# Taking GpSimd out of block 2's recurrent branch and attention on one Trainium2 core

## The chip, the cores and the metric

The kernel runs on one core of one Trainium2 chip. The metric is the device time of one execution in microseconds. TensorE (PE) does matmuls and transposes, VectorE (DVE) and ScalarE (ACT) do element-wise work and read PSUM, GpSimd (POOL) does element-wise work on SBUF, and SyncE (SP) issues DMAs. Each engine works through its own queue in order.

## The reference, cut to what matters

Two first blocks (a pooled branch and latent attention) and one second block run over 512 tokens of width 1024; 16 meta tokens are added for the first two blocks. The change lies in the second block, in the recurrent branch and in the differential attention:

```python
# recurrent branch, for each direction (forward, reverse)
r = sigmoid(x @ w_a + b_a); i = sigmoid(x @ w_i + b_i)
log_a = -8 * r * softplus(-lam)
a = exp(log_a)
u = sqrt(-expm1(2 * log_a)) * (i * x)
h = scan(h = a * h + u);  y = (h_fwd + h_bwd) * gelu(lru_g)
# attention: 8 heads, two sub-heads of 64 each
q = rope(rms_norm(q)); k = rope(rms_norm(k))
p = softmax(q0 k0 / 8) - lam * softmax(q1 k1 / 8)
o = rms_norm(p @ v) * (1 - lam_init)
# then: gates * (o @ w_attn_o, y @ w_lru_o), w_out, and a mixture of 16 experts
```

## The kernel before, in words

**Precision.** Every fp32 product is made of three matmuls: the operands are split into a rounded high part (a cast on ScalarE, L145 for weights, names `wh`, `xH`) and a low part (a subtraction on VectorE, L146, names `wl`, `xL`); `mm3` (L151 to L153) issues high x high, high x low, low x high. Outputs land in PSUM tiles `mm`.

**Order.** The program is written as one stream, and the framework's list scheduler orders each engine's queue ahead of time, by priority and by its own idea of when operands are ready. Buffers of a pool are handed out in turn, so a new tile waits until the old one in its buffer has been read. Independent projections are written as Python generators of steps (`fill`), and `next(fill)` puts a step of them between pieces of the recurrent branch and of the attention. Below they are called fillers: matmuls that PE can do while a chain through other engines is under way.

**The recurrent branch** (L1011 to L1055) runs in 4 groups of 2 units. A unit splits its input `xr` into `rH` (ScalarE) and `rL` (VectorE, L1024), computes four gate products into PSUM (`sc`, `tr`, `pv`), and then, in each of two directions: Tanh of both gates (L1034, L1035), Exp to the decay `la` (L1036), another Tanh (L1037), the square of the decay `a2` (L1039, GpSimd), and (a2 + 1) * m2 on VectorE (L1040). L1041 makes the input term. A group ends with the square roots on ScalarE (L1047, behind a load of the function table), and with L1049, two scans (L1050, L1051) and the sum of both directions `hs` (L1052, GpSimd) on each unit. The fillers here are the steps of `qkv2` for heads 0 to 3 and of `lru_g` (L1003 to L1008).

**qkv2** (L1240 to L1286) computes k, q and v for four heads. For each 128 tokens of k and q, ScalarE squares the PSUM result, VectorE sums (L1264), multiplies by the rotary cosine (L1265, `kt` or `qt`) and by the sine with halves exchanged (L1266, `rt`), and GpSimd adds both (L1270). The PSUM bank is free after L1266.

**Attention** (L1288 to L1357) goes over 8 heads, in two rounds of four. A head transposes k and q (L1304, PE, into PSUM `tr`) and splits them: ScalarE copies the high part (L1306, 64 partitions at a time), VectorE subtracts the low part (L1308, `kl` or `q`). For k, both parts are needed on the other 64 partitions too: GpSimd copies `kh` (L1310) and `kl` (L1311) across. Then, for each of four blocks of 128 queries: scores of two sub-heads (L1326, L1327, PSUM `sc`), the maximum (L1328), Exp with a running sum (L1330), the combination (L1331 to L1333), the transposition of the probabilities (L1336) and its copy `pT` (L1338), the product with v (L1340, PSUM `pv`), its scaling `ot` (L1341) and its squares `junk` (L1343). The head ends with a norm over the four blocks (L1346 to L1348, with the 11 small VectorE instructions of `rsqrt`, L169 to L176), a transposition (L1350) and the split of `o` (L1353, L1354). `ps_tr` and `ps_pv` have one bank each; `ps_sc` has two in the first round and four in the second. Fillers of the first round are `lru_o` (operands `lH`, `lL`) and qkv2 for heads 4 to 7; of the second, the gates `g_lru` and `g_attn` (operands `x2H`, `x2L`). Behind the last head come `w_attn_o` (`mm<-o`), `w_out`, the router and the experts.

Of the kernel before, what the change touches and what calls it, by code (L numbers as in the profile page):

```python
# [11 lines left out]
F32 = mybir.dt.float32  # L12
# [4 lines left out]
AF = mybir.ActivationFunctionType  # L17
ALU = mybir.AluOpType
AX = mybir.AxisListType

P = 128
D = 1024
KD = D // P
SEQ = 512
# [110 lines left out]
class Builder:  # L135
# [779 lines left out]
    def block2(self, xH, xL, squares, out):  # L915
        nc, A, tc = self.nc, self.A, self.tc
        V, S, E = nc.vector, nc.scalar, nc.tensor
        with ExitStack() as ctx:
# [15 lines left out]
            sp = sm.tile([P, 16], F32, name="sp")  # L934
# [15 lines left out]
            V.tensor_scalar(t, t, 0.0, 0.5, op0=ALU.max, op1=ALU.mult)  # L950
            V.tensor_tensor(sp, sp, t, op=ALU.add)
            spm = {}
            for f in (-8.0, 8.0):
                spm[f] = sm.tile([P, 16], F32, name=f"sp{int(f) + 16}")
                V.tensor_scalar(spm[f], sp, f, None, op0=ALU.mult)
            hb = {}
            for w in ("a", "i"):
# [37 lines left out]
            hs = Later(self, "hs", 8, SEQ)  # L995
# [18 lines left out]
            for grp in range(4):  # L1014
                wH, wL = [t.rearrange("p (n m c) -> p n m c", n=2, m=4) for t in wl.get(grp)]
                units = []
                for nn in range(2):
                    n = 2 * grp + nn
                    rH = med.tile([P, SEQ], F32R, name="rH", tag="hl")
                    rL = med.tile([P, SEQ], F32R, name="rL", tag="hl")  # L1020
                    ix = med.tile([P, 2, SEQ], F32, name="ix", tag="pr")
                    a, m2 = self.pair("la", F32, (P, 2, SEQ)), self.pair("lm", F32, (P, 2, SEQ))
                    S.copy(rH, xr[n])
                    V.tensor_tensor(rL, xr[n], rH.bitcast(F32), op=ALU.subtract)  # L1024
                    for dd in range(2):
                        u = 8 * dd + n
                        if dd == 0:
                            pr, pi = [self.ps_sc.tile([P, SEQ], F32, name="sc") for _ in range(2)]
                        else:
                            pr = self.ps_tr.tile([P, SEQ], F32, name="tr")  # L1030
                            pi = self.ps_pv.tile([P, SEQ], F32, name="pv")
                        self.mm3(pr, wH[:, nn, 2 * dd], wL[:, nn, 2 * dd], rH, rL, True, True)
                        self.mm3(pi, wH[:, nn, 2 * dd + 1], wL[:, nn, 2 * dd + 1], rH, rL, True, True)
                        S.activation(m2[:, dd], pr, AF.Tanh, scale=0.5, bias=hb["a"][:, u:u + 1])  # L1034
                        S.activation(ix[:, dd], pi, AF.Tanh, scale=0.5, bias=hb["i"][:, u:u + 1])  # L1035
                        S.activation(a[:, dd], m2[:, dd], AF.Exp, scale=spm[-8.0][:, u:u + 1], bias=spm[-8.0][:, u:u + 1])  # L1036
                        S.activation(m2[:, dd], m2[:, dd], AF.Tanh, scale=spm[8.0][:, u:u + 1], bias=spm[8.0][:, u:u + 1])  # L1037
                        a2 = med.tile([P, SEQ], F32, name="a2", tag="pT", bufs=2)
                        nc.gpsimd.tensor_tensor(a2, a[:, dd], a[:, dd], op=ALU.mult)  # L1039
                        V.scalar_tensor_tensor(m2[:, dd], a2, 1.0, m2[:, dd], op0=ALU.add, op1=ALU.mult)  # L1040
                    V.scalar_tensor_tensor(ix, ix, 1.0, xr[n][:, None, :].to_broadcast([P, 2, SEQ]),  # L1041
                                           op0=ALU.add, op1=ALU.mult)
                    units.append((n, a, m2, ix))
                zero = sm.tile([P, 1], F32, name="zero", bufs=2)
                V.tensor_scalar(zero, units[-1][2][:, 1, :1], 0.0, None, op0=ALU.mult)
                for n, a, m2, ix in units:
                    S.activation(m2, m2, AF.Sqrt, scale=0.25, bias=zero)  # L1047
                for n, a, m2, ix in units:
                    V.tensor_tensor(ix, ix, m2, op=ALU.mult)  # L1049
                    V.tensor_tensor_scan(hs[n], a[:, 0], ix[:, 0], 0.0, op0=ALU.mult, op1=ALU.add)  # L1050
                    V.tensor_tensor_scan(m2[:, 1, ::-1], a[:, 1, ::-1], ix[:, 1, ::-1], 0.0, op0=ALU.mult, op1=ALU.add)  # L1051
                    nc.gpsimd.tensor_tensor(hs[n], hs[n], m2[:, 1], op=ALU.add)  # L1052
                for _ in range(5 if grp < 2 else 4):
                    next(fill, None)

# [173 lines left out]
    def qkv2(self, b, wi, xH, xL, inv, epsx, out):  # L1229

        nc = self.nc
        V, S = nc.vector, nc.scalar
        sm, med = self.sm, self.med
        if b == 0:
            self.rope2_tables()
        for w in ("k", "q", "v"):
            tl = []
            for j in range(0, 4, 2):
                t = self.pair(w + "t", F32, (P, 2, SEQ))
                tl += [t[:, 0], t[:, 1]]  # L1240
            out[w] = tl
            pss = [self.psum() for _ in range(4)]
            for i in range(4):
                wH, wL = [t.rearrange("p (k c) -> p k c", k=2) for t in wi[w].get(4 * b + i)]
                for j in range(4):
                    ts = slice(j * P, (j + 1) * P)
                    for kk in range(2):
                        k = 2 * i + kk
                        self.mm3(pss[j], xH[k][:, ts], xL[k][:, ts], wH[:, kk], wL[:, kk], k == 0, k == KD - 1)
                if i < 3:  # L1250
                    yield
            if w != "v":
                ss = sm.tile([P, 4, 8], F32, name="ss" + w)
            for j in range(4):
                ps = pss[j]
                if w == "v":
                    S.activation(tl[j], ps, AF.Copy, scale=inv[:, j:j + 1])
                    continue
                sq = med.tile([P, SEQ], F32, name="sq_", tag="th")
                rt = med.tile([P, SEQ], F32, name="rt_", tag="z", bufs=3)  # L1260
                p8 = ps.rearrange("p (s c) -> p s c", s=8)
                t8 = tl[j].rearrange("p (s c) -> p s c", s=8)
                S.activation(sq, ps, AF.Square)
                V.tensor_reduce(ss[:, j], sq.rearrange("p (s c) -> p s c", s=8), axis=AX.X, op=ALU.add)  # L1264
                V.tensor_tensor(t8, p8, self.TC2[w][:, j, None, :].to_broadcast([P, 8, 64]), op=ALU.mult)  # L1265
                V.tensor_tensor(rt.rearrange("p (s h c) -> p s h c", s=8, h=2),  # L1266
                                ps.rearrange("p (s h c) -> p s h c", s=8, h=2)[:, :, ::-1],
                                self.TS2[w][:, j].rearrange("p (h c) -> p h c", h=2)[:, None].to_broadcast([P, 8, 2, 32]),
                                op=ALU.mult)
                nc.gpsimd.tensor_tensor(tl[j], tl[j], rt, op=ALU.add)  # L1270
            if w == "v":
                yield
                continue
            r = sm.tile([P, 4, 8], F32, name=f"r{w}{b}")
            V.scalar_tensor_tensor(ss, ss, 1.0 / 64, epsx[:, :, None].to_broadcast([P, 4, 8]), op0=ALU.mult, op1=ALU.add)
            self.rsqrt(r, ss, [P, 4, 8], sm)
            if w == "q":
                V.tensor_scalar(r, r, 0.125, None, op0=ALU.mult)
                out["f"] = r
            else:  # L1280
                for j in range(4):
                    t8 = tl[j].rearrange("p (s c) -> p s c", s=8)
                    V.tensor_tensor(t8, t8, r[:, j, :, None].to_broadcast([P, 8, 64]), op=ALU.mult)
            yield

    def attention2(self, b, qkv, lneg, gs, out):  # L1286
# [4 lines left out]
        nc = self.nc  # L1291
        V, S, E = nc.vector, nc.scalar, nc.tensor
        sm, med = self.sm, self.med
        qt, kt, vt, rq = qkv["q"], qkv["k"], qkv["v"], qkv["f"]
        halves = (slice(0, 64), slice(64, P)), (slice(64, P), slice(0, 64))
        for hh in range(4):
# [4 lines left out]
            for src, t2 in ((kt, KH), (qt, QS)):  # L1301
                pt = self.ps_tr.tile([P, SEQ], F32, name="tr")
                for j in range(4):
                    E.transpose(pt[:, j * P:(j + 1) * P], src[j][:, hh * P:(hh + 1) * P], self.ident)  # L1304
                for c, (own, other) in enumerate(halves):
                    S.copy(t2[own, c], pt[own])  # L1306
                    low = KL[c][own] if t2 is KH else t2[other, c]
                    V.tensor_tensor(low, pt[own], t2[own, c].bitcast(F32), op=ALU.subtract)  # L1308
                    if t2 is KH:
                        nc.gpsimd.tensor_copy(t2[other, c], t2[own, c])  # L1310
                        nc.gpsimd.tensor_copy(KL[c][other], low)  # L1311
            po = self.ps_pv.tile([P, 4, P], F32, name="pv")
            ot = med.tile([P, 4, P], F32, name="ot")
            so = sm.tile([P, 4], F32, name="so", bufs=2)
# [515 lines left out]
```

## Time and profile before

| | |
|---|---|
| median of 3 runs | 1806.4 us (1805.15 to 1806.85) |
| profiled execution, its own time | 1805.66 us |
| its span | 1803.9 us |
| PE busy | 1737.3 us, 96% |
| VectorE busy | 1215.6 us, 67% |
| ScalarE busy | 926.4 us, 51% |
| GpSimd busy | 263.1 us, 15% |

The span is the time between the first and the last instruction that the profile shows; 1.76 us of the execution lie around it. Busy shares are averages over stages with different limits. The recurrent branch lies between 940 and 1092 us of the span, the heads between 1090 and 1388 us, and the experts fill 1520 to 1750 us. A listed duration of an instruction is a little longer than the distance between two that follow each other without a gap, since their ends overlap; a sum over a queue goes by the distance. A wait is put down to the engine and line that released it last.

### The profile page before, as it was taken

The page shows a single profiled execution, that of the slowest core. Times are in us where ns is not written, and L with a number is a line of the kernel's source. Part 1 is how long each engine was busy: PE and PEld are TensorE (multiplying, and loading weights), DVE is VectorE, ACT ScalarE, POOL GpSimd, SP SyncE. Part 2 cuts the span into 40 slices and gives each one's busy share as a digit, 9 for nine tenths or more (in the row PEclk, how much of TensorE's full clock was granted, in tenths as well). Part 3 has the DMA queues.
Part 4 walks back from the last instruction along what each step waited for, and adds up shares of the span by engine and source line. Part 5 has one row for each costly group of instructions (what it writes and reads, how often), then busy time and mean ns, then how long its engine had stood idle before and what let it go on. Part 6 is the DMA issues. An engine that isn't in the chain of part 4 may idle for free. (4 is left out here: it accounts for less than half of the span.)

```text
span 1803.9 us, 25746 instructions
## 1 busy us (share of the span) xinstructions
PE 1737.3 (96%) x9706; PEld 1464.3 (81%) x9706; DVE 1215.6 (67%) x2265; ACT 926.4 (51%) x1546; POOL 263.1 (15%) x255
## 2 busy tenths in 40 slices
PE   7999999999999999999999899999999997999997
PEld 7889899999976888888877677777787886888885
DVE  7485555456357555446598988586776539999996
ACT  5343244434434334433337665545565335888885
POOL 4102400001210320000203321021101031111111
PEclk9999999999999999999999999999999998999999
DMA  4122111223322122213532221222124568999995
GB/s 146 59 89 71 49 56 67 77 77 136 116 77 93 53 71 69 72 61 101 181 108 71 82 93 71 70 70 71 47 71 163 190 210 300 383 384 386 381 383 161
DMA packets 69089, 244.36 MB, mean 135 GB/s; under 512 B 10848, under 2 KB 20064, under 8 KB 57056
## 3 DMA queue, kind: packets, MB, share of 16 engines
q1 hardware_dynamic: 64352, 225.89, 34.6%
q0 software_dynamic: 4608, 16.78, 3.7%
q8 instruction: 78, 1.28, 0.3%
q14 instruction: 51, 0.42, 0.1%
HBM read 225.20 MB, written 17.37 MB: 134 GB/s over the span
## 5 line engine op out<-in xcount | busy, mean ns | idle before, releaser
L145 ACT CAST wh<-raw 128x1024 fp32r<-128x1024 f32 (+2 forms) x206 | 212.3, 1031 | 412.9 <-PE mm L152 332.3
L146 DVE TENSOR_TENSOR wl<-raw,wh 128x1024 fp32r<-128x1024 f32 (+2 forms) x206 | 253.6, 1232 | 101.7 <-ACT wh L145 99.8
L151 PE MATMUL mm<-xH,wh 128*128 128x264 f32 (+1 forms) x912 | 291.3, 320 | 11.5 <-ACT xH L361 9.4
L152 PE MATMUL mm<-xL,wh 128*128 128x264 f32 (+1 forms) x912 | 291.1, 320 | 1.3 <-DVE xL L362 1.3
L153 PE MATMUL mm<-xH,wl 128*128 128x264 f32 (+1 forms) x912 | 290.0, 319 | 0.0
L146 DVE TENSOR_TENSOR wl<-we,wh 128x1024 fp32r<-128x1024 f32 x192 | 227.5, 1221 | 15.2 <-ACT wh L145 13.6
L145 ACT CAST wh<-we 128x1024 fp32r<-128x1024 f32 x192 | 198.6, 1050 | 47.6 <-PE mm L153 30.3
L151 PEld LDWEIGHTS mm<-xH,wh 128*128 128x128 f32 x912 | 173.7, 191 | 24.7 <-ACT xH L361 9.4
L152 PEld LDWEIGHTS mm<-xL,wh 128*128 128x128 f32 x912 | 173.9, 191 | 12.2 <-DVE xL L362 2.2
L153 PEld LDWEIGHTS mm<-xH,wl 128*128 128x128 f32 x912 | 173.9, 191 | 10.3
L151 PE MATMUL mm<-wh,eH 128*128 128x512 f32 x256 | 104.2, 407 | 0.0
L151 PE MATMUL mm<-x2H,wh 128*128 128x512 f32 x256 | 102.2, 399 | 0.0
L152 PE MATMUL mm<-x2L,wh 128*128 128x512 f32 x256 | 101.9, 398 | 0.0
L153 PE MATMUL mm<-x2H,wl 128*128 128x512 f32 x256 | 101.8, 398 | 0.0
L153 PE MATMUL mm<-wh,eL 128*128 128x512 f32 x256 | 101.0, 395 | 0.0
L152 PE MATMUL mm<-wl,eH 128*128 128x512 f32 x256 | 100.7, 393 | 0.0
L126 POOL TENSOR_TENSOR z<-z,sq 128x528 f32<-128x528 f32 (+1 forms) x26 | 43.4, 1670 | 331.1 <-DVE wl L146 230.7
L151 PE MATMUL mm<-wh,x2H 128*128 128x512 f32 x192 | 77.0, 402 | 4.8 <-DVE rt__9342 L1266 2.8
L153 PE MATMUL mm<-wh,x2L 128*128 128x512 f32 x192 | 76.1, 400 | 0.0
L152 PE MATMUL mm<-wl,x2H 128*128 128x512 f32 x192 | 76.1, 396 | 0.0
L789 ACT ACTIVATE pr<-sc,bi,r3q 128x264 f32<-128x264 f32 (+3 forms) x80 | 46.6, 590 | 54.9 <-DVE bi L787 54.2
L151 PE MATMUL mm<-mgH,wh 128*128 128x264 f32 (+1 forms) x192 | 61.7, 321 | 0.0
(625 smaller groups left out, 4051.6 us busy)
## 6 DMA issues: line engine op xcount, KB each, us to landing
we<-in_w_moe SPq DMA_DIRECT2D x192, 512.0 KB
raw<-in_w_out SPq DMA_DIRECT2D x12, 1024.0 KB
raw<-in_w_g_mla SPq DMA_DIRECT2D x8, 1024.0 KB
raw<-in_w_g_pool SPq DMA_DIRECT2D x8, 1024.0 KB
raw<-in_w_c_q SPq DMA_DIRECT2D x6, 1024.0 KB
raw<-in_w_q_b SPq DMA_DIRECT2D x6, 768.0 KB
raw<-in_w_z_mla SPq DMA_DIRECT2D x4, 1024.0 KB
raw<-in_w_u_pool SPq DMA_DIRECT2D x4, 1024.0 KB
```

Source lines behind the costliest of these rows:

```text
L126: self.kb.nc.gpsimd.tensor_tensor(self.sum[:, off:], self.sum[:, off:], sq[:, off:], op=ALU.add)
L145: nc.scalar.copy(H[:, :F], src)
L146: lo.tensor_tensor(L[:, :F], src, H[:, :F].bitcast(F32), op=ALU.subtract)
L151: mm(out, lH, rH, start=start, stop=False)
L152: mm(out, lH, rL, start=False, stop=False)
L153: mm(out, lL, rH, start=False, stop=stop)
L789: S.activation(pr[:, a:b, e], scs[q], AF.Exp, bias=bi[:, e:e + 1], scale=c, accum_out=su[:, e, q:q + 1])
```

## The change

72 instructions leave GpSimd; 32 are added on ScalarE and 41 on VectorE:

- L1039: the square of the decay (16 times) becomes a second Exp on ScalarE, with the scale -16 in the place of -8 (a third small table column `sp`, made once).
- L1052: the sum of both directions (8 times) goes to VectorE.
- L1270: the sum of both rotary products (16 times) goes to VectorE.
- L1310: the copy of the high keys to the other partitions (16 times) becomes a second ScalarE copy from PSUM.
- L1311: the copy of the low keys (16 times) becomes a second VectorE subtraction from PSUM.

```diff
-            for f in (-8.0, 8.0):
+            for f in (-16.0, -8.0, 8.0):
...
+                        a2 = med.tile([P, SEQ], F32, name="a2", tag="pT", bufs=2)
+                        S.activation(a2, m2[:, dd], AF.Exp, scale=spm[-16.0][:, u:u + 1], bias=spm[-16.0][:, u:u + 1])
                         S.activation(m2[:, dd], m2[:, dd], AF.Tanh, scale=spm[8.0][:, u:u + 1], bias=spm[8.0][:, u:u + 1])
-                        a2 = med.tile([P, SEQ], F32, name="a2", tag="pT", bufs=2)
-                        nc.gpsimd.tensor_tensor(a2, a[:, dd], a[:, dd], op=ALU.mult)
...
-                    nc.gpsimd.tensor_tensor(hs[n], hs[n], m2[:, 1], op=ALU.add)
+                    V.tensor_tensor(hs[n], hs[n], m2[:, 1], op=ALU.add)
...
-                nc.gpsimd.tensor_tensor(tl[j], tl[j], rt, op=ALU.add)
+                V.tensor_tensor(tl[j], tl[j], rt, op=ALU.add)
...
-                    low = KL[c][own] if t2 is KH else t2[other, c]
-                    V.tensor_tensor(low, pt[own], t2[own, c].bitcast(F32), op=ALU.subtract)
+                    for low in (KL[c][own], KL[c][other]) if t2 is KH else (t2[other, c],):
+                        V.tensor_tensor(low, pt[own], t2[own, c].bitcast(F32), op=ALU.subtract)
                     if t2 is KH:
-                        nc.gpsimd.tensor_copy(t2[other, c], t2[own, c])
-                        nc.gpsimd.tensor_copy(KL[c][other], low)
+                        S.copy(t2[other, c], pt[own])
```

From L1310 on, the changed kernel's line numbers are one lower. The scheduler orders the queues anew. The order on PE is another between the recurrent branch and the end of the attention, with the same matmuls, and the same before and behind that.

VectorE at the end of the recurrent branch's first group, where the scans are followed by the evacuation of k (`ssk`, `kt`, `rt`). Before:

```order
L1050 SCALAR_TENSOR_TENSOR hs_9192<-la_9114,ix 128x512
L1051 SCALAR_TENSOR_TENSOR lm_9115<-la_9114,ix 128x512
L146 TENSOR_TENSOR wl<-raw,wh 128x1024
L1050 SCALAR_TENSOR_TENSOR hs_9192<-la_9152,ix 128x512
L1051 SCALAR_TENSOR_TENSOR lm_9153<-la_9152,ix 128x512
L1264 TENSOR_REDUCE ssk<-sq__9341 128x8
L1265 TENSOR_TENSOR kt_9218<-mm,TC2k 128x512
L1266 TENSOR_TENSOR rt__9342<-mm,TS2k 128x512
L1264 TENSOR_REDUCE ssk<-sq__9348 128x8
L1265 TENSOR_TENSOR kt_9218<-mm,TC2k 128x512
```

Now, at the same place:

```order
L1052 TENSOR_TENSOR hs_9194<-hs_9194,lm_9117 128x512
L1050 SCALAR_TENSOR_TENSOR hs_9194<-la_9154,ix 128x512
L146 TENSOR_TENSOR wl<-raw,wh 128x1024
L1051 SCALAR_TENSOR_TENSOR lm_9155<-la_9154,ix 128x512
L1264 TENSOR_REDUCE ssk<-sq__9343 128x8
L1052 TENSOR_TENSOR hs_9194<-hs_9194,lm_9155 128x512
L1265 TENSOR_TENSOR kt_9220<-mm,TC2k 128x512
L1266 TENSOR_TENSOR rt__9344<-mm,TS2k 128x512
L1264 TENSOR_REDUCE ssk<-sq__9350 128x8
L1270 TENSOR_TENSOR kt_9220<-kt_9220,rt__9344 128x512
L1265 TENSOR_TENSOR kt_9220<-mm,TC2k 128x512
```

Two sums (L1052) stand ahead of the instruction that frees the first bank (L1266), and a sum (L1270) between each bank and the next.

PE where head 0 ends and head 1 begins: the last product with v, the transpositions of the next keys (`kt`), and the transposition of head 0's output (`pv<-ident,ot`). Before:

```order
L1340 MATMUL pv<-vt_9653,pT 128x128 x2
L1304 MATMUL tr<-ident,kt_9218 128x128 x2
L1304 MATMUL tr<-ident,kt_9219 128x128 x2
L153 MATMUL mm<-lH_9912,wl 128x512
L151 MATMUL mm<-lH_10089,wh 128x512
L152 MATMUL mm<-lL_10091,wh 128x512
...
L153 MATMUL mm<-lH_10171,wl 128x512
L151 MATMUL mm<-lH_10397,wh 128x512
L1350 MATMUL pv<-ident,ot 128x128 x4
```

Now:

```order
L153 MATMUL mm<-lH_10399,wl 128x512
L1339 MATMUL pv<-vt_9654,pT 128x128 x2
L1339 MATMUL pv<-vt_9655,pT 128x128 x2
L1304 MATMUL tr<-ident,kt_9220 128x128 x2
L1304 MATMUL tr<-ident,kt_9221 128x128 x2
L1349 MATMUL pv<-ident,ot 128x128 x4
L151 MATMUL mm<-lH_9914,wh 128x512
```

The 14 fillers between the transpositions of the keys and that of the output now stand elsewhere, and none is left between them.

PE in the last head (head 7), between the transposition of its queries (`qt`) and its first products with v. Before, a piece of it:

```order
L1304 MATMUL tr<-ident,qt_11210 128x128 x2
L152 MATMUL mm<-x2L_8393,wh 128x512
...
L152 MATMUL mm<-x2L_8394,wh 128x512
L1326 MATMUL sc<-kh_12766,q_12769 128x512
L1327 MATMUL sc<-kl_12767,q_12769 128x512
L153 MATMUL mm<-x2H_8390,wl 128x512
...
L1336 MATMUL tr<-ident,pr 128x128 x4
L1326 MATMUL sc<-kh_12766,q_12769 128x512
L1327 MATMUL sc<-kl_12768,q_12769 128x512
L153 MATMUL mm<-x2H_8390,wl 128x512
```

Now:

```order
L1304 MATMUL tr<-ident,qt_11212 128x128 x2
L1325 MATMUL sc<-kh_12768,q_12771 128x512
L1326 MATMUL sc<-kl_12769,q_12771 128x512
...
L1325 MATMUL sc<-kh_12768,q_12771 128x512
L1326 MATMUL sc<-kl_12770,q_12771 128x512
L1335 MATMUL tr<-ident,pr 128x128 x4
L1339 MATMUL pv<-vt_11470,pT 128x128 x2
L1339 MATMUL pv<-vt_11471,pT 128x128 x2
L1335 MATMUL tr<-ident,pr 128x128 x4
L1339 MATMUL pv<-vt_11470,pT 128x128 x2
```

Before, 41 fillers (`mm<-x2H` and `mm<-x2L`) stand between this head's query transposition and its last product with v. Now there is none: all 16 score matmuls follow each other, the first transposition of probabilities stands behind the last of them, and 8 and 16 matmuls of `w_attn_o` (`mm<-o`) come before and behind the head's last product with v. The 41 are spread over heads 3 to 6.

## Rows read from the trace of the kernel before

**Rows 1.** The page: busy time by engine, and the chain that ended last.
```profile
PE 1737.3 (96%) x9706; PEld 1464.3 (81%) x9706; DVE 1215.6 (67%) x2265; ACT 926.4 (51%) x1546; POOL 263.1 (15%) x255
...
PE 39%; DVE 6%; ACT 1%; issue 1%; DMA 0%; POOL 0%; POOLq 0%; DVEq 0%; ACTq 0%
```

**Rows 2.** PE's waits, 930 to 1112 us: line, releaser; total, times, longest.
```profile
PE sc L152 <- DVE rL L1024: 3.8, 3, 1.7
PE tr L1304 <- DVE kl L1308: 2.8, 1, 2.8
PE mm L151 <- DVE rt__9342 L1266: 2.8, 1, 2.8
PE sc L151 <- ACT wh L145: 2.3, 2, 1.1
PE mm L151 <- DVE rt__9608 L1266: 2.0, 1, 2.0
PE sc L153 <- DVE wl L146: 1.3, 1, 1.3
PE mm L151 <- ACT lH L1007: 0.8, 1, 0.8
PE mm L152 <- DVE lL L1008: 0.3, 1, 0.3
```

**Rows 3.** Windows: length, busy PE, PEld, DVE, ACT, POOL, granted clock, DMA share, GB/s.
```profile
960.00:980.00 20.00, 17.23 (x75) 13.51 (x74) 20.00 (x23) 12.09 (x17) 10.57 (x8) 1.00 0.30 105
...
1003.00:1015.00 12.00, 8.75 (x31) 6.75 (x32) 12.00 (x16) 7.94 (x12) 7.57 (x8) 0.86 0.25 89
1090.00:1106.00 16.00, 12.10 (x47) 9.10 (x46) 15.64 (x26) 10.27 (x18) 4.32 (x4) 0.89 0.17 65
...
1366.00:1388.00 22.00, 22.00 (x121) 17.59 (x120) 16.69 (x37) 16.90 (x39) 3.32 (x4) 1.00 0.31 104
```

**Rows 4.** VectorE's timeline, 956 to 982 us: start, us, instruction.
```profile
961.76 1.22 DVE L1050 TENSOR_TENSOR_SCAN hs<-la,ix 128x512 f32<-128x512 f32 x1
...
965.12 2.31 DVE L1050 TENSOR_TENSOR_SCAN hs<-la,ix 128x512 f32<-128x512 f32 x1
...
969.05 0.68 DVE L1265 TENSOR_TENSOR kt<-mm,TC2k 128x512 f32<-128x512 f32 x1
969.65 0.68 DVE L1266 TENSOR_TENSOR rt__9342<-mm,TS2k 128x512 f32<-128x512 f32 x1
...
977.65 2.37 DVE L1041 SCALAR_TENSOR_TENSOR ix<-ix,xr 128x1024 f32<-128x1024 f32 x1
```

**Rows 5.** GpSimd's timeline, beside the slow scan.
```profile
964.26 2.10 POOL L1052 TENSOR_TENSOR hs<-hs,lm 128x512 f32<-128x512 f32 x1 [8.72 <-PE mm L153]
```

**Rows 6.** ScalarE's groups by line: busy us, mean ns of one, idle before.
```profile
L1330 ACT ACTIVATE pr<-sc,bi,rq 128x512 f32<-128x512 f32 x64 | 49.5, 778 | 14.7 <-DVE bi L1329 14.7
L1338 ACT COPY pT<-tr 128x512 f32<-128x512 f32 x32 | 18.7, 584 | 18.5 <-PE tr L1336 18.4
L1036 ACT ACTIVATE la<-lm,sp 128x512 f32<-128x512 f32 x16 | 12.9, 814 | 0.0
...
L1306 ACT CAST kh<-tr 64x512 fp32r<-64x512 f32 x16 | 9.2, 577 | 4.6 <-DVE kl L1308 4.5
```

**Rows 7.** PE's timeline where head 0 ends.
```profile
1121.31 0.60 PE L1304 MATMUL tr<-ident,kt 128*128 128x128 f32 x4
...
1124.54 0.40 PE L153 MATMUL mm<-lH,wl 128*128 128x512 f32 x1
1124.77 0.39 PE L151 MATMUL mm<-lH,wh 128*128 128x512 f32 x1
1125.57 0.63 PE L1350 MATMUL pv<-ident,ot 128*128 128x128 f32 x4 [0.41 <-DVE ot L1348]
```

**Rows 8.** PE's timeline: the last head's query transposition, and what follows its last product.
```profile
1367.75 0.63 PE L1304 MATMUL tr<-ident,qt 128*128 128x128 f32 x4
...
1387.18 0.48 PE L151 MATMUL mm<-o,wh 128*128 128x512 f32 x1
```

More of the change, by code (lines that the diff above doesn't have):

```diff
@@ L952, in block2 @@
             spm = {}
-            for f in (-8.0, 8.0):
-                spm[f] = sm.tile([P, 16], F32, name=f"sp{int(f) + 16}")
+            for f in (-16.0, -8.0, 8.0):
+                spm[f] = sm.tile([P, 16], F32, name=f"sp{int(f) + 16}_")
                 V.tensor_scalar(spm[f], sp, f, None, op0=ALU.mult)
```

## The prediction

> **What bounds the kernel now.** I read the page's busy shares and its chain of waits first, then PE's waits by stretch, then the windows, and last the timelines of the places where the order on PE changes. PE is busy for 96% of the span, and GpSimd has 0% of the chain that ended last [rows 1]. So GpSimd's own time buys nothing: an edit counts only where PE stands still, or will. The list of PE's waits shows where that is inside the changed part: between 930 and 1112 us PE waits eight kinds of waits long, 3.8 + 2.8 + 2.8 + 2.3 + 2.0 + 1.3 + 0.8 + 0.3 = 16.1 us [rows 2]. The releasers there are VectorE and ScalarE, and in the window 960 to 980 VectorE is busy all of its 20.00 us [rows 3]. The stalls also cost clock: the granted clock is 0.86 of full speed in 1003 to 1015 and 0.89 in 1090 to 1106, where PE was busy 8.75 of 12 and 12.10 of 16 us, and 1.00 elsewhere [rows 3]. Full speed is 2.4 GHz and the lower level 1.2, so at most 0.14 x 12 + 0.11 x 16 = 3.4 us are lost to it. All that the change could win here is 16.1 + 3.4 = 19.5 us. In the attention behind it there is next to nothing to win: in the last head's window PE is busy 22.00 of 22 us [rows 3].
>
> **Part 1, recurrent branch and heads' start (940 to 1112 us).** GpSimd's instructions cost VectorE time though nothing waits for them: a scan takes 1.22 us alone and 2.31 us beside GpSimd's sum of 2.10 us [rows 4, 5]. L1041 with 1024 columns takes 2.37 us in such company [rows 4]. VectorE instructions with both inputs in SBUF are stretched so; those that read PSUM (L1265, L1266) stay at 0.68. I counted 16 such instructions in its timeline from 940 to 1097 (the two named are among them), each about 1 us over its undisturbed twin: some 16 us of VectorE time, 7.4 of it in the packed stretch 956 to 1021.
>
> Against that, VectorE gets 8 sums L1052 and 8 sums L1270 here. None is in the trace on VectorE; the nearest rows are L1265 and L1266, of the same size, 0.60 us apart [rows 4]. 16 x 0.60 = 9.6 us, with the two low keys of head 0 (half the partitions, about 0.6 each) 10.8 us, of which 7.2 lie in 956 to 1021. There the two cancel; in the whole stretch VectorE comes out 5 us lighter. ScalarE gets 16 more Exps, each 0.81 us listed [rows 6], some 0.71 in a full queue: 11.4 us, and each group's four stand ahead of its square roots, so 2.8 us per group stand ahead of the root, the scans, and the weights' cast L145 queued behind.
>
> I walked the new queues from group to group with these durations. The rL waits (3.8 us) shrink to about 0.6, since rL is no longer stretched; the first rt wait, 2.8, becomes 0.8, but 1.3 comes ahead of it at wl; the two waits for the cast (2.3) become 4.2, because more Exps stand ahead of it; the second rt wait, 2.0, becomes 5.9, since two sums and the later square root now stand ahead of q's first bank; the 3.9 us at lH, lL and the first head's transpositions become 0.3, since more lru_o matmuls (37 instead of 18) stand ahead of head 0's queries and no GpSimd copy stands behind kl. With 1.4 of clock that is 0.6 + 0.8 + 1.3 + 4.2 + 5.9 + 0.3 + 1.4 = 14.5 against 19.5: a gain of 5 us. The bounds are a gain of 15 (the walk is too dark by two thirds, and only the casts' 4.2 stay) and a loss of 3 (rt and the casts each worse by 4).
>
> The Trainium skill's page "SBUF — State Buffer", section "Who interferes with whom", states the cause: a VectorE instruction with two SBUF inputs and a GpSimd instruction that reads SBUF need the same port pair, and the second is blocked for the whole of the first; a VectorE instruction with at most one SBUF input isn't. The trace agrees (2.31 against 1.22 us for the scan, 0.68 for L1265 beside GpSimd) [rows 4]. By that rule all of the 16 us come back, which is rival A below.
>
> **Part 2, end of head 0.** Before, 14 fillers lie between the transpositions of head 1's keys and that of head 0's output; PE starts the former at 1121.31 and the latter at 1125.57, after a wait of only 0.41 us [rows 7]. The chain in between (ot, junk, twelve small VectorE instructions, ot again) doesn't touch GpSimd and stays as long. Now no filler is there, so PE stands for it: 14 x 0.23 us (the distance of two matmuls [rows 7]) = 3.2 us more, 3.5 with the re-start. The fillers run earlier, in places where PE was already full, and save nothing there. Bounds: 2 and 4.
>
> **Part 3, heads 1 to 6.** ScalarE gets two copies per head, 0.58 us each [rows 6], VectorE two subtractions of about 0.69 and half of the L1270 sums. Fillers cover these: 94 to 99 of them now stand in each of heads 3 to 6. Only at head 3, where the scores now follow the queries' transposition at once, do I book 0.5 us. If the cover were too thin, two ScalarE copies a head would cost up to 1.2 us x 6 = 7; if the keys came earlier without GpSimd, it would win at most the 0.9 us or so that PE waits here. I take 0.5.
>
> **Part 4, the last head.** Before, 19.43 us pass from the queries' transposition at 1367.75 to the first matmul behind the last product with v at 1387.18 [rows 8], without a gap, and 41 fillers fill 41 x 0.23 = 9.5 us of it. Now it has no filler, and 8 matmuls of w_attn_o (1.9 us) in their place. How long is the bare chain? ScalarE sets it: about 4.2 us until the first Exp (transposition, copy, low part, scores, maximum), eight Exps of 0.78, four pT of 0.58 [rows 6], four ot and junk of 0.9 together. That is 4.2 + 6.2 + 2.3 + 2.7 (the last ot and junk lie behind) = 15.4. To it come about 1.2 us between the first and second Exp, 1.1 because the first transposition of probabilities waits behind the last score matmul (whose bank is freed by the fourth Exp), and 1.1 for the last pT and product: 18.8 us. So the head costs 18.8 - 19.4 + 9.5 - 1.9 = 7.0 us of PE time. Bounds: 5 (chain of 16.8) and 10 (clock halved for 3 us beside the gaps, as [rows 3] shows it after a PE busy for three quarters).
>
> Behind it, w_attn_o, w_out, router and experts keep their order and PE stays the bound, so they only shift.
>
> **Sum.** -5 + 3.5 + 0.5 + 7.0 = +6.0 us on the profiled execution's 1805.66 (its span 1803.9 and 1.76 around it): 1811.7. The median of the runs shown, 1806.4, is 0.7 higher, so I say 1812.
>
> **Rivals.**
>
> A, faster: the end of the stretching decides. If VectorE's 16 us all arrive at the places where PE waits, the 19.5 us go, and the tail costs 11.0: 1805.7 - 19.5 + 11.0 = 1797. For it: six of the eight kinds of waits end at VectorE, 13.0 us of the list [rows 2]. Against it: the sums that were GpSimd's now stand in the same queue ahead of L1266, and ScalarE has more to do ahead of the casts. It decides (by more than 0.2%, about 3.6 us) from the point where less than 19.5 - 11.0 - 3.6 = 5 us of stalls and lost clock remain in 940 to 1112.
>
> B, no change: the gain is larger (10 us) and the tail just pays it back, 1805.7 - 10 + 11 = 1806.7. For it: stalls of a few us each, any of which the walk can have wrong by 2. Against it: the 8 us or more of bare chain at the end of head 0 and in the last head are certain from the order alone.
>
> C, slower still: no gain in the recurrent branch (q's banks and the casts late behind the added Exps, +3 instead of -5), and the last head with the halved clock (+10): 1805.7 + 3 + 3.5 + 0.5 + 10 = 1823. For it: PE fell to the lower clock at both deep stalls [rows 3], and a last head without fillers has PE busy little over half. Against it: VectorE as a whole gets lighter.
>
> **How the numbers follow.** Measurement can tell a change of about 0.2%, 3.6 us. Forecast (+3.6 to +12 us) 0.48, A 0.17, B 0.23, C 0.12. So faster 0.17, same 0.23, slower 0.48 + 0.12 = 0.60. The likeliest case's own range is 1809.5 to 1818. For 8 in 10 the range takes in B and the nearer half of A and of C: 1800 to 1820.
>
> **What would show it.** In the new trace: L1050 and L1041 at 1.2 us everywhere; PE's waits in 930 to 1112 near 13 us with a long one at q's L1266; a wait of about 4 us at the transposition of head 0's output; and 7 to 8 us of gaps in the last head, with PE busy there some 60% and perhaps a lower granted clock. Wrong would be: gaps of less than 3 us in the last head (then other work covers it), or stalls under 5 us in the recurrent branch (then A).

## The result and the profile after

The changed kernel takes 1823.96 us (median of 4 runs, 1822.59 to 1828.02) against 1806.58 (4 runs): 17.4 us or 1.0% more, ratio 1.0100 with a 95% interval of 1.0087 to 1.0114. It is slower, as forecast, but by nearly three times the 6 us of the sum, and above the range's end of 1820. Its profiled execution has a span of 1820.6 us, 16.7 over that of before.

The page after, busy time by engine:

```profile
PE 1747.1 (96%) x9706; PEld 1469.6 (81%) x9706; DVE 1223.9 (67%) x2306; ACT 946.6 (52%) x1578; POOL 180.6 (10%) x183
```

PE does the same 9706 matmuls, yet it is busy 9.8 us longer than in [rows 1]. Only the other 6.9 of the 16.7 us are time in which PE does nothing. The windows say why (same columns as [rows 3]; the column behind POOL's is the granted clock):

```profile
960.00:980.00 20.00, 16.81 (x66) 13.08 (x65) 20.00 (x31) 11.93 (x18) 0.00 (x0) 0.91 0.29 105
...
1000.00:1020.00 20.00, 14.98 (x50) 11.12 (x49) 17.93 (x27) 9.52 (x15) 0.00 (x0) 0.74 0.16 52
...
1110.00:1130.00 20.00, 15.06 (x87) 11.88 (x86) 13.17 (x32) 12.61 (x30) 0.00 (x0) 0.93 0.29 106
1130.00:1180.00 50.00, 49.59 (x233) 39.22 (x233) 25.53 (x56) 25.24 (x53) 0.00 (x0) 0.96 0.19 64
...
1220.00:1260.00 40.00, 36.21 (x167) 28.39 (x166) 29.32 (x72) 19.75 (x40) 0.00 (x0) 0.96 0.15 53
...
1388.00:1420.00 32.00, 27.98 (x131) 21.04 (x132) 20.07 (x58) 15.92 (x38) 1.97 (x10) 0.95 0.55 206
```

The granted clock is below 1.00 in six windows; before, it was 1.00 in all of these except 1000 to 1020. Before, it fell to 0.91 there and in 1090 to 1110:

```profile
1000.00:1020.00 20.00, 15.65 (x59) 12.04 (x60) 20.00 (x27) 10.37 (x14) 11.42 (x8) 0.91 0.27 100
1090.00:1110.00 20.00, 16.10 (x67) 12.29 (x66) 19.20 (x37) 13.00 (x24) 4.32 (x4) 0.91 0.14 52
```

In 1090 to 1110 it is 1.00 now. Where it falls, matmuls follow each other every 0.43 us (the lower of the two levels, 1.2 GHz) instead of 0.23. In the part of PE's timeline whose order changes, 45 matmuls of 512 columns take 0.42 us or more to the next one with no wait between, against 11 before. At 0.23 us each they would take 9.4 and 2.5 us less, so they make up some 7 of the 9.8 us. PE's timeline at the end of head 0, which answers to [rows 7], shows a wait, then slow matmuls, then the old pace:

```profile
1123.10 0.60 PE L1304 MATMUL tr<-ident,kt 128*128 128x128 f32 x4
1127.38 1.08 PE L1349 MATMUL pv<-ident,ot 128*128 128x128 f32 x4 [3.68 <-DVE ot L1347]
1129.71 0.80 PE L151 MATMUL mm<-lH,wh 128*128 128x512 f32 x1 [1.25 <-ACT gp L1061]
1130.31 0.63 PE L152 MATMUL mm<-lL,wh 128*128 128x512 f32 x1
1130.73 0.63 PE L153 MATMUL mm<-lH,wl 128*128 128x512 f32 x1
...
1134.41 0.39 PE L153 MATMUL mm<-lH,wl 128*128 128x512 f32 x1
1134.64 0.39 PE L151 MATMUL mm<-lH,wh 128*128 128x512 f32 x1
...
1137.66 0.60 PE L1304 MATMUL tr<-ident,qt 128*128 128x128 f32 x4
```

The last head, which answers to [rows 8]: waits for q and, further on, for pT, no fillers, and score matmuls at 0.43 us behind the waits. The last line is the window of the whole head, to be held against the last one of [rows 3].

```profile
1385.26 0.62 PE L1304 MATMUL tr<-ident,qt 128*128 128x128 f32 x4
1388.30 0.50 PE L1325 MATMUL sc<-kh,q 128*128 128x512 f32 x1 [2.43 <-DVE q L1308]
...
1390.54 0.80 PE L1325 MATMUL sc<-kh,q 128*128 128x512 f32 x1 [1.51 <-DVE q L1308]
1391.13 0.63 PE L1326 MATMUL sc<-kl,q 128*128 128x512 f32 x1
1391.56 0.63 PE L1325 MATMUL sc<-kh,q 128*128 128x512 f32 x1
...
1406.19 0.48 PE L153 MATMUL mm<-o,wl 128*128 128x512 f32 x1
...
1385.00:1407.00 22.00, 16.25 (x82) 11.49 (x81) 13.09 (x32) 13.79 (x36) 0.53 (x1) 0.92 0.26 86
```

PE's waits in 930 to 1112 us, against [rows 2]: the rL waits are gone, and new ones, at ScalarE, stand in their place. The sum is 12.7 us (16.1 before), but more is lost by the clock.

```profile
PE sc L151 <- ACT wh L145: 4.0, 2, 2.9
PE sc L151 <- ACT rH L1023: 3.2, 1, 3.2
PE mm L151 <- DVE rt__9610 L1266: 2.5, 1, 2.5
PE sc L151 <- ACT ix L1035: 2.5, 1, 2.5
PE mm L151 <- ACT lH L1007: 0.5, 1, 0.5
```

**A ledger by place.** At each head's query transposition I took the delay against the kernel before, and subtracted 0.232 us (the distance of two matmuls at full clock) for each matmul by which the new order is ahead there. Two points of it, before:

```profile
927.26 0.40 PE L151 MATMUL mm<-x2H,wh 128*128 128x512 f32 x1
...
1096.23 1.09 PE L1304 MATMUL tr<-ident,qt 128*128 128x128 f32 x4 [2.82 <-DVE kl L1308]
```

and now:

```profile
925.05 0.40 PE L151 MATMUL mm<-x2H,wh 128*128 128x512 f32 x1
...
1097.74 0.66 PE L1304 MATMUL tr<-ident,qt 128*128 128x128 f32 x4
```

The first line of each is PE's 5701st matmul, ahead of the recurrent branch, where both kernels still have the same order. This execution of the changed kernel is already 2.2 us early there. That is no gain of the branch: the traces of all fourteen kernels, which share the order up to here, pass this matmul anywhere between 925.05 and 928.93 us. At head 0 the changed kernel is 1.5 us late but 19 matmuls ahead, 2.9 us to the good; without the 2.2 us, the recurrent branch won 0.7. Three runs below (e4, e5, e9) have the changed kernel's order up to this place, and their traces give 0.7 as well. At head 1 it is 5.65 us late and 6 ahead: 7.2 us lost between the two. At heads 2 and 3 the balance hardly moves (-0.2, -0.4); head 3 loses 3.3, heads 4 to 6 together 1.0. At the transposition of head 7's output it is 18.8 us late and 6 matmuls ahead: 9.4 lost in the last head. -0.7 + 7.2 - 0.6 + 3.3 + 1.0 + 9.4 = 19.6 us. The spans differ by only 16.7, since the 2.2 us ahead of the branch and 0.7 behind PE's last matmul go the other way.

The medians differ by 17.4. For all 13 changed versions (this one and e1 to e12) the traces' difference in this part of PE's timeline is 0.3 to 3.4 us above the medians' difference, so the one trace of the kernel before probably ran it some 2 us faster than its usual run. In which place is not shown: one term of the ledger may be too high by that, and the branch's gain may be up to 3 us.

### The profile page after: what moved, and what is told of

Same layout as the page of the kernel before. It is cut to its first block, busy times and chain, and to the rows that moved or that the text cites. A ratio compares the mean times of both kernels' runs of the same rounds, so it can differ in the third digit from the quotient of the medians.

```text
span 1820.6 us, 25652 instructions
## 1 busy us (share of the span) xinstructions
PE 1747.1 (96%) x9706; PEld 1469.6 (81%) x9706; DVE 1223.9 (67%) x2306; ACT 946.6 (52%) x1578; POOL 180.6 (10%) x183
## 4 chain that ended last, share of the span: by engine, by line
PE 87%; DVE 7%; ACT 4%; issue 1%; DMA 1%; POOL 0%; SPq 0%; POOLq 0%; ACTq 0%; DVEq 0%
PE mm L151 24%; PE mm L153 24%; PE mm L152 24%; PE pv L819 2%; PE sc L781 2%; DVE wl L146 2%; PE pv L1339 1%; PE tr L806 1%; PE sc L1325 1%; ACT wh L145 1%; PE tr L1562 1%; PE sc L1326 1%; PE tr L1335 1%; PE sc L554 1%; PE pv L813 1%
## 5 line engine op out<-in xcount | busy, mean ns | idle before, releaser
L145 ACT CAST wh<-raw 128x1024 fp32r<-128x1024 f32 (+2 forms) x206 | 212.0, 1030 | 403.3 <-PE mm L152 322.1
L146 DVE TENSOR_TENSOR wl<-raw,wh 128x1024 fp32r<-128x1024 f32 (+2 forms) x206 | 251.5, 1223 | 109.4 <-ACT wh L145 107.6
L146 DVE TENSOR_TENSOR wl<-we,wh 128x1024 fp32r<-128x1024 f32 x192 | 227.3, 1220 | 15.7 <-ACT wh L145 13.3
L145 ACT CAST wh<-we 128x1024 fp32r<-128x1024 f32 x192 | 198.5, 1050 | 47.9 <-PE mm L153 33.8
L1329 ACT ACTIVATE pr<-sc,bi,rq 128x512 f32<-128x512 f32 x64 | 49.4, 777 | 31.1 <-DVE bi L1328 31.1
```

The lines of the kernel that those rows point to most:

```text
L145: nc.scalar.copy(H[:, :F], src)
L146: lo.tensor_tensor(L[:, :F], src, H[:, :F].bitcast(F32), op=ALU.subtract)
L1329: S.activation(pr[:, c], sc, AF.Exp, bias=bi[:, c1], scale=cc[:, c1], accum_out=su[:, c1])
```

## The experiments

Each comparison is with runs of the kernel before on the same chip, whose median lay between 1806.8 and 1807.3 us in them. A difference between two changed versions is one of medians from different rounds; by the ratios to before it comes out up to 2 us larger or 1 smaller.

**e1, only the copies of the keys.** The line pairs L1310 and L1311 alone are changed:

```diff
+                    for low in (KL[c][own], KL[c][other]) if t2 is KH else (t2[other, c],):
+                        V.tensor_tensor(low, pt[own], t2[own, c].bitcast(F32), op=ALU.subtract)
...
-                        nc.gpsimd.tensor_copy(t2[other, c], t2[own, c])
-                        nc.gpsimd.tensor_copy(KL[c][other], low)
+                        S.copy(t2[other, c], pt[own])
```

> Only the copies of the high and low keys leave GpSimd (second ScalarE copy and second VectorE subtraction from PSUM); squares and sums stay on GpSimd. Bank theory: the single PSUM bank of the key and query transpositions is now read by four copies and four subtractions before it is free, so the queries' transposition comes later, 30 fillers stand ahead of it in each head, and the last head has none left. That alone costs about 9 us in the last head, 6 at the end of head 0 (2 fillers left) and 1 in heads 5 and 6: 1820 to 1823 us. Rival, load theory (the added sums and Exps on VectorE and ScalarE in the recurrent branch are the cost): within 4 us of before, 1804 to 1810.

Measured: 1825.20 us, ratio 1.0102 (1.0086 to 1.0119). The copies alone cost as much as the whole change, more than either theory said (2.2 us above the bank theory's range). The load theory falls: 32 of the 73 added instructions, of half width, bring the whole loss.

**e2, the copies stay on GpSimd, the rest is changed.**

> Squares and sums leave GpSimd, the copies of the keys stay on it. Bank theory: heads 1 to 7 have the fillers of before, so no gap in the last head; what is left is the recurrent branch (the trace of the changed kernel has it at about -1 us against before) and 3 instead of 14 fillers at the end of head 0 (+3 us or more, with lost clock): 1805 to 1811 us. Load theory: most of the 17 us is here, 1818 or more.

Measured: 1810.94 us, ratio 1.0019 (1.0010 to 1.0029), inside what the bank theory said. PE's wait at the end of head 0 is there (4.0 us), the last head has no gap.

**e3, all four edits, but the copies read SBUF.** The transposition's bank is then free after two copies and two subtractions, as before:

```diff
-                        nc.gpsimd.tensor_copy(t2[other, c], t2[own, c])
-                        nc.gpsimd.tensor_copy(KL[c][other], low)
+                        S.copy(t2[other, c], t2[own, c])
+                        V.tensor_copy(KL[c][other], low)
```

> All four edits, but the copies of the keys to the other partitions read SBUF as on GpSimd before (ScalarE copies kh from kh, VectorE copies kl from kl), so the transposition's PSUM bank is free after two copies and two subtractions. GpSimd does as little as in the changed kernel, and ScalarE and VectorE have as many instructions. Bank theory: heads 1 to 7 keep their fillers (33 in the last head), the loss in the last head (9 us), head 3 (3.6) and heads 5 and 6 (1.3) goes: 1807 to 1812 us. Load theory: as the changed kernel, 1820 to 1826.

Measured: 1813.56 us, ratio 1.0031 (1.0020 to 1.0042): 10.4 less than the changed kernel with the same number of instructions on each engine, though 1.6 above my upper bound. The expectation took 9 + 3.6 + 1.3 = 13.9 us off; the ledger of e3's trace is 11.9 below that of the changed kernel, with the 9.0 in the last head but less than expected in heads 3 to 6. The end of head 0, with 2 fillers, still loses 7.4. The window of e3's last head, which runs from 1375.89 us on:

```profile
1376.00:1398.00 22.00, 21.77 (x119) 17.62 (x119) 16.69 (x41) 16.17 (x40) 0.53 (x1) 1.00 0.39 123
```

PE is busy 21.77 of 22 us at full clock, where the changed kernel had 16.25 at 0.92.

**e4, the changed kernel with two banks for transpositions** in the second round of heads:

```diff
-            self.ps, self.ps_sc, self.ps_tr, self.ps_pv = self.banks(banks, "ps2b", 2, 4, 1, 1)
+            self.ps, self.ps_sc, self.ps_tr, self.ps_pv = self.banks(banks, "ps2b", 2, 3, 2, 1)
```

> All four edits as in the changed kernel, but the second round of heads has two PSUM banks for transpositions and three for scores (instead of one and four). Bank theory: the queries' transposition needs not wait for the keys' bank, the fillers ahead of it go (none instead of 30), and the last head has about 94 of them: its loss of 9 us goes, the losses in the recurrent branch and at the end of head 0 stay: 1811 to 1817 us. Load theory: 1820 to 1826.

Measured: 1816.44 us, ratio 1.0050 (1.0033 to 1.0067), as the bank theory said: 7.5 us less than the changed kernel. With e3 this shows the cause in the last head. The group rows of the changed kernel show how the bank is held longer:

```profile
L1310 ACT CAST kh<-tr 64x512 fp32r<-64x512 f32 x16 | 9.3, 582 | 13.3 <-DVE kl L1308 13.1
```

Each second copy waits for the subtractions ahead of it (13.1 us over 16 copies), so that a half of the keys goes through ScalarE, VectorE twice, and ScalarE again, where it went through each once. Behind head 6 the queries' transposition came 10.5 us after that of the keys (1357.22 to 1367.75); now it comes 11.9 after (1373.36 to 1385.26). In the order, 30 fillers stand between the transposition of a head's output and that of the next queries, where 18 to 22 stood, in each of heads 3 to 6, and the scheduler runs out of them: the last head has none. In e4 none stand there, and the last head has 96.

**e5, the clock.** The changed kernel, and 13 matmuls of no use in the gap at the end of head 0. Every other instruction on PE keeps its place:

```diff
+            if h == 0:
+                for _ in range(13):
+                    E.matmul(po.rearrange("p j c -> p (j c)"), KH[:, 0, :P], KH[:, 0], start=True, stop=True)
             V.tensor_scalar(so, so, 1.0 / P, EPS, op0=ALU.mult, op1=ALU.add)
```

> The changed kernel plus 13 matmuls of no use (128x512, into a bank that is overwritten behind them) where head 0 ends, between the transpositions of head 1's keys and that of head 0's output, where PE waits 3.7 us; every other instruction on PE keeps its place. Clock theory (a good half of what the changed kernel loses beyond the waits is that PE falls to the lower clock after a wait and does the following matmuls at half speed): the wait is filled, the granted clock stays at 1.00 in 1110 to 1180 where it was 0.93 and 0.96, and the kernel is 2 to 4 us faster, though PE has 13 matmuls more: 1820 to 1822 us. Rival (the clock in the record costs nothing, waits are all): no gain, 1823 to 1825 us.

Measured: 1822.04 us, ratio to before 1.0081 (1.0067 to 1.0095); the changed kernel's own ratio was 1.0100. That is 1.9 us less with 13 matmuls more; the two intervals overlap, so the total alone settles nothing. The trace of the place does. PE's timeline of e5:

```profile
1124.00 0.60 PE L1304 MATMUL tr<-ident,kt 128*128 128x128 f32 x4
1124.62 3.24 PE L1347 MATMUL pv<-kh 128*128 128x512 f32 x13
1128.20 0.66 PE L1352 MATMUL pv<-ident,ot 128*128 128x128 f32 x4 [0.34 <-DVE ot L1350]
1130.12 0.50 PE L151 MATMUL mm<-lH,wh 128*128 128x512 f32 x1 [1.25 <-ACT gp L1061]
1130.45 0.40 PE L152 MATMUL mm<-lL,wh 128*128 128x512 f32 x1
...
```

and its windows (the third has most of the last head):

```profile
1110.00:1130.00 20.00, 18.50 (x102) 14.38 (x101) 13.72 (x35) 13.11 (x33) 0.00 (x0) 1.00 0.31 106
1130.00:1180.00 50.00, 49.45 (x240) 39.28 (x241) 26.39 (x57) 26.80 (x56) 0.00 (x0) 1.00 0.19 64
...
1388.00:1420.00 32.00, 29.28 (x135) 22.30 (x136) 19.30 (x56) 15.46 (x37) 1.98 (x10) 0.90 0.57 219
```

The second wait is still 1.25 us, but the matmuls behind it run at the fast pace from the first on, and the granted clock is 1.00 in the first two windows. From the keys' to the queries' transposition it is 12.0 us (1124.00 to 1136.01) against 14.6 in the changed kernel: 2.5 us at this place were clock, and nothing but clock. Part of that went again in the last head, where the granted clock is 0.90 in the third window with the same order on PE (0.95 in the changed kernel).

**e6 to e8, the other edits one by one**, each as in the change's diff: L1270 alone, L1052 alone, L1039 alone.

> Only the sums of the rotary products (L1270) move from GpSimd to VectorE. The order on PE is that of before up to head 2 and hardly differs behind it, so this weighs 0.60 us per sum on VectorE against the stretching by GpSimd in the same stretch. Contention theory: VectorE gets as much back as it takes on, PE's waits for rt and rL stay or shrink: 1803 to 1807.5 us. Load theory: the sums stand ahead of the next bank's release, waits for rt grow by 2 to 4 us: 1809 to 1812 us.

> Only the sums of both scan directions (L1052) move from GpSimd to VectorE. At the end of head 0, 6 fillers are left of 14. Contention theory: the scans run at 1.2 us, waits before 1070 us shrink by about 1 us, the end of head 0 costs 2 us and some clock: 1806 to 1810 us. Load theory: the sums delay rt in both groups as well: 1811 or more.

> Only the squares of the decays (L1039) become Exps on ScalarE; 5 fillers are left at the end of head 0. If the Exps are what brings the new waits of the changed kernel in the recurrent branch (rH 3.2, wh 2.9, ix 2.5 us, with a granted clock of 0.74 in 1000 to 1020): 1809 to 1814 us with these waits. If the sums on VectorE bring them: the branch is as before or better and only the end of head 0 costs 2 to 4 us: 1806 to 1810 us.

Measured: rotary sums 1804.96 us, ratio 0.9992 (0.9983 to 1.0001); scan sums 1807.66, ratio 1.0003 (0.9994 to 1.0012); squares 1808.72, ratio 1.0012 (1.0003 to 1.0021). The sums make no difference that can be told; the squares cost some 2 us, inside what was expected (1806 to 1810) if the Exps as such cost nothing. In the last two, PE waits 3.3 and 3.5 us at the end of head 0, since 6 and 5 fillers are left there of 14. By the ledger on their traces, e7 and e8 lose 6.7 and 6.1 us at that place and win 2.8 and 1.7 in the recurrent branch, so the loss of e8 is not in the branch, where its Exps stand. With the copies of e1 the four ratios add up to 1.0109, and the whole was 1.0100; that is luck, since e1, e7 and e8 each contain the loss at the end of head 0 that the whole has once.

**e9, the changed kernel with fillers put back at the end of head 0.** The steps are handed out earlier:

```diff
-                for _ in range(2 if step >= 2 else 0):
+                for _ in range((0, 1, 2, 1)[step] if step < 4 else 2):
```

> The changed kernel, with the steps of the fillers between the first heads handed out as 1, 2, 1 and then 2 each, where they were 0, 2, 2: 14 fillers stand again between the transpositions of head 1's keys and that of head 0's output; heads 3 to 7 keep the changed kernel's order. Theory (the end of head 0 costs 3.3 us of wait, 1.1 more behind it, and 2.6 of lost clock): 1815 to 1819 us, and the granted clock is 1.00 in 1110 to 1180. Rival (the wait moves to the next place that has too few fillers): 1822 to 1825 us.

Measured: 1818.86 us, ratio 1.0062 (1.0049 to 1.0075): 5.1 us less than the changed kernel. The granted clock is 1.00 in 1110 to 1180, and the second wait of 1.25 us is gone as well. The wait did not move on.

**e10 to e12, the mended versions.** All have e9's edit. e10 is e3 with it, e11 is e2 with it, e12 has the sums alone on VectorE.

> All four edits, the copies of the keys reading SBUF, and the fillers' steps handed out as 1, 2, 1: both places that lost their fillers (the last head and the end of head 0) have them again, and GpSimd does nothing in this part. Theory: what is left is the recurrent branch, about equal to before, so 1805 to 1809 us. Rival (work on VectorE and ScalarE as such costs time): 1811 us or more.

> Squares and sums off GpSimd, the copies of the keys on it as before, the fillers' steps handed out as 1, 2, 1, so that 19 fillers stand at the end of head 0 (3 without that). Theory: 7 us less than with 3 fillers there (1810.9): 1803 to 1806 us. Rival (the 3 us over before are the Exps' waits in the recurrent branch): 1809 us or more.

> Only the sums (L1052, L1270) on VectorE, squares and copies on GpSimd, the fillers' steps handed out as 1, 2, 1. Theory: the recurrent branch gains 2 to 4 us from undisturbed scans and the end of head 0 costs nothing: 1800 to 1804 us, faster than before. Rival (contention of VectorE and GpSimd was not what cost time, only the order matters): 1806 to 1808 us, as before.

Measured: e10 1806.72 us, ratio 0.9999 (0.9990 to 1.0008); e11 1803.68, ratio 0.9984 (0.9975 to 0.9992); e12 1802.97, ratio 0.9983 (0.9975 to 0.9992), each inside its theory's range. So GpSimd can be left out of this part at no cost that can be told (e10, with as many instructions on ScalarE and VectorE as the changed kernel), and two versions beat the kernel before by about 3 us (the intervals run from 1.4 to 4.5). e11 is 7.3 below e2, and e10 6.8 below e3: that is what the end of head 0 costs, measured twice more. The ledger on every run's trace agrees: the end of head 0 loses 6.1 to 7.4 us in each version that has 0 to 6 fillers there (e5, with its useless matmuls, apart), and at most 1.0 in those with 14 or 19; the last head loses 8.6 to 9.9 where the copies read PSUM and there is one bank, and at most 1.0 elsewhere. The waits of e12 in 930 to 1112 us still hold 15 us in sum; three of them:

```profile
PE sc L151 <- ACT wh L145: 3.4, 2, 2.3
PE mm L151 <- DVE rt__9608 L1266: 3.3, 1, 3.3
PE sc L151 <- ACT ix L1035: 2.5, 1, 2.5
```

## Why the prediction was wrong

The direction and the two places without fillers were right, each term's size was not: the sum +6.0 had -5, +3.5, +0.5 and +7.0 where the ledger has -0.7, +7.2, +3.7 and +9.4. Of the signs named, the scans at 1.2 us, the waits near 13 us and the wait of about 4 us came; the wait at q's L1266 was 2.5 us and not the longest, and the last head's gaps were 5.75 of 22 us, not 7 to 8, with PE busy 74% of the time at a granted clock of 0.92.

**Recurrent branch: -5 forecast, -0.7 found.** The walk's waits came to 13.1 us, the trace has 12.7, though not where I put them: rt at q's first bank is 2.5 and not 5.9, while waits at rH (3.2) and at ix (2.5), which I had not foreseen, stand beside the casts' 4.0. The scans and L1024 run at 1.2 and 0.68 us again, as predicted. What failed is the clock, of which the sum left 1.4 us from 3.4: 0.91 in 960 to 980 and 0.74 in 1000 to 1020 make 1.8 + 5.2 = 7.0 us lost at most, where before 0.91 in two windows made 3.6. Counted by the slow matmuls it is 4.6 us now and 2.5 before. The waits shrank by 3.4 us and the clock took back 2.1 to 3.4.

**End of head 0: +3.5 forecast, +7.2 found.** The wait is 3.68 us, as priced. Behind it come a second wait, 1.25 us for a bank that ScalarE evicts late (a consequence of the missing fillers, which I didn't look at: in e9, where they are back, it is gone), and about ten matmuls at 0.43 us, 2 us, with the output's transposition slowed as well. e5 measured the clock's part, 2.5 us.

**Heads 1 to 6: +0.5 forecast, +3.7 found,** nearly all of it in head 3, where I had seen that the scores follow the queries' transposition at once, but priced the wait at 0.5 us above before's 0.9. It is 2.56 and 0.81 us, with the clock at 0.96 behind it:

```profile
1247.66 0.50 PE L1325 MATMUL sc<-kh,q 128*128 128x512 f32 x1 [2.56 <-DVE q L1308]
...
1249.90 0.52 PE L1325 MATMUL sc<-kh,q 128*128 128x512 f32 x1 [0.81 <-DVE q L1308]
```

**Last head: +7.0 forecast, +9.4 found.** The chain was priced at 18.8 us up to the first matmul behind the last product with v; the trace has 1385.26 to 1406.19, 20.9 us. The 2.1 us lie at the start, as ScalarE's first two Exps show:

```profile
1390.71 0.78 ACT L1329 ACTIVATE pr<-sc,bi,rq 128x512 f32<-128x512 f32 x1 [1.85 <-DVE bi L1328]
...
1393.44 0.78 ACT L1329 ACTIVATE pr<-sc,bi,rq 128x512 f32<-128x512 f32 x1 [1.87 <-DVE bi L1328]
```

The first comes 5.5 us after the transposition began, where 4.2 was priced (a cast and a split of weights, L145 and L146, stand ahead of q on ScalarE and VectorE); the second comes 2.7 behind it, where about 2.0 was priced, with score matmuls at half speed in between.

So the main step that failed in the sum is one: I charged waits as waits, with 1.4 us for the halved clock in the recurrent branch and nothing elsewhere. Besides that I had it only in the last head's upper bound and in rival C, at +3. Counted by the slow matmuls, the clock took 4.6 us in the branch (2.5 before), 2.1 at the end of head 0 (2.5 with the output's transposition, by e5), 1.4 in head 3 and 1.3 in the last head. That is about 9 of the 13.6 us by which the ledger lies above the sum. The rest are waits that I had not priced or priced too low: the 1.25 us at the end of head 0, those of head 3, and the last head's slow start. Rival C's total (1823) came close to the measured time, but that is luck: it had the recurrent branch at +3, where 0.7 was won, and the last head at +10 (9.4), and both other places too low.

Rival A is refuted but its mechanism is real: L1050 runs at 1.2 us without GpSimd beside it. Its group before, then now:

```profile
L1050 DVE TENSOR_TENSOR_SCAN hs<-la,ix 128x512 f32<-128x512 f32 x8 | 11.9, 1488 | 0.0
```

```profile
L1050 DVE TENSOR_TENSOR_SCAN hs<-la,ix 128x512 f32<-128x512 f32 x8 | 9.7, 1215 | 0.0
```

With the order mended, e11 and e12 are faster than before, by about 3 us rather than by 9. By the rule cited from the Trainium skill ("SBUF — State Buffer", "Who interferes with whom") the blocked time comes back, and the trace agrees: 1.215 us on the mean of the eight L1050, 1.488 before. It did not decide: of PE's 12.7 us of waits in the branch, 10.2 now end at ScalarE (wh, rH, ix, lH), where 3.1 of 16.1 did before.

One thing stays open: in e6 to e12 a change of what waits (contention) comes together with a change of the order on PE. How much of what e12 gained is VectorE undisturbed and how much is a luckier order was not separated; e6, whose order differs least, is inside its uncertainty. Nor do the traces place the gain where e12's expectation had it: by the ledger its recurrent branch is 0.4 us slower than before's (e11's 1.0 faster).

## What to carry to other kernels

Moving work off an idle engine can lengthen the hold of a shared buffer: a copy that read SBUF and now reads PSUM keeps the bank, and the scheduler answers by spending its fillers there. Look in the new order for the place where the fillers run out, not at the engine loads. And price a wait of PE by the wait and the slower matmuls behind it: at the end of head 0 waits of 3.7 and 1.25 us brought 2.5 us of slower matmuls with them, and filling the first gap with useless matmuls made the stretch shorter. Before a gain is credited to a stretch, compare both traces at a point ahead of it where the orders still agree.

## What the runs showed of the hardware that was not expected

After waits of 3.7 and 1.25 us, with PE busy for 1 us between them, the matmuls behind ran every 0.43 us for some 4.5 us before the pace came back; with 13 useless matmuls in the first wait, and the second unchanged, not one ran slowly. What the clock takes at a place is not settled by the order alone: in the last head, with the same order on PE, 6 matmuls ran slowly in the changed kernel, 11 in e5 and 12 in e9. The recurrent branch, in contrast, repeats closely: from the 5701st matmul to head 0's query transposition it took 172.66 to 172.71 us in the four traces that share the changed kernel's order.
